# Retention's values by seven products instead of eight, with stored operand sums, in a two-block transformer kernel

## Chip, core and metric

The kernel runs on one NeuronCore of a Trainium2 chip. The metric is the time of one execution on the device in microseconds (us). PE is the matmul engine, ACT the scalar engine, DVE the vector engine, POOL the GpSimd engine; SP is the engine whose queue issues nearly all DMAs.

## What is computed

Two transformer blocks run over 512 tokens of width 1024 in fp32, and all large products are with weights that are read from HBM. Block 1 (a hybrid mixer and a feed-forward network, "ffn" here) stands ahead of the change. Block 2 has two layers of this form:

```python
mod = c_act @ w_ada + b_ada                      # "ada": per layer 3 rows of 1024
shift, scale, gate = jnp.split(mod, 3, axis=-1)
h = rmsnorm(x, norm_w) * (1.0 + scale[:, None, :]) + shift[:, None, :]
qa, ka, va, za, qr, kr, vr, zr, ga, gr = jnp.split(h @ w_in, SPLIT_POINTS, axis=-1)
# va: 3 groups of 512 columns, values of dilated attention; vr: 1024 columns, values of retention
...
o_ret = retention(qr, kr, vr, positions, ret_gn_w)   # rotary(q), rotary(k), chunks of 128 tokens
merged = sigmoid(ga) * (y_att @ w_proj_attn) + sigmoid(gr) * (o_ret * silu(zr) @ w_proj_ret)
return x + gate[:, None, :] * (merged @ w_out)
```

## The kernel before

Every fp32 operand is held as two parts, hi (rounded by ACT) and lo (the rest, by DVE), and each product of tiles is three matmuls: hi·hi, hi·lo and lo·hi. `load_w` (L188) brings one weight tile of 128x1024 (512 KB): a DMA on SP's queue into a raw buffer (L193; two in the ordinary pool, four more while a stage lends its own), ACT's split to `wh` (L144) and DVE's to `wl` (L145). A weight serves 24 matmuls of 512 columns in the products that matter here.

The program is written out by Python code in which tasks (`spawn`) take turns with the main line: after each step of a product the main line lets tasks run that are due by a clock of modelled matmul time (a task's `pace`). A scheduler then fixes the order of the instructions on each engine, SP's queue too, and weight loads are given a higher priority there. Each queue runs in its fixed order.

The stages of a block-2 layer, in order: `strided_v` gives the values of the second and third attention group; `attention` follows, which begins with the query and key weights ("qk"); then `retention_v`, the projection `pa`, `retention`, and the gates and the output.

`strided_v` (L1059) already multiplies by `TS_` (L311), a scheme of Strassen and Winograd: the product of 512 tokens, 1024 inputs and two groups of 512 columns is cut into halves of tokens and of inputs, and seven products of halves take the place of eight. It wants sums of the halves of the operand `h` (tiles `H`, four pairs of hi and lo, made in `strided_v` from `h`) and sums of the weights (`weight_sums`, L364: loads `q`, four operations on POOL, stores to HBM). The results `X` are laid into the attention's `V` tiles by 32 small DMAs (L1092), 8 first and 24 at the end. The weight sums of layer 0 are made as a task in the ffn of block 1, those of layer 1 in the last part of layer 0 (`rt2`).

`retention_v` (L1259) in contrast is an ordinary product of 8 weights, called twice a layer: the first half of the columns ahead of `pa`, the second inside `retention`. The rotary tables (`rotary_tables`, L1014; DVE work and two ACT operations that each change ACT's function table) are made in layer 0's `attention`, next to the join of its heads.

`ada` (L647) is a task in the ffn: 12 half rows, for each 8 weight pieces `aw` of 256 KB that DVE accumulates (L660), then two matmuls against a matrix of ones sum over the partitions.

Of the kernel before, what the change touches and what calls it, by code (L numbers as in the profile page):

```python
# [50 lines left out]
class Block:  # L51
# [309 lines left out]
        product("b", Sx(2), Tx(2), False, p7)  # L361
        product("a", Sx(3), B(1, 1), True, p3)

    def weight_sums(self, src, dst, pool, pace):  # L364

        g = self.nc.gpsimd
        for i in range(2):
            for o in (slice(0, 512), slice(512, D)):
                q = []
                for half, c in ((0, i), (1, i), (1, 2 + i), (0, 2 + i)):  # L370
                    q.append(pool.tile([P, 512], F32, tag=f"q{len(q)}", name=self.nm("q"), bufs=1))
# [12 lines left out]
    def all_weight_sums(self, l, pool, pace):  # L384
        A = self.A
        for n, src in (("va", [A["w2_va"][l, g] for g in (1, 2)]),):
            self.w_sums[n, l] = self.dp.tile([8, P, D], F32, tag=f"{n}{l}", name=f"{n}{l}")
            yield from self.weight_sums(src, self.w_sums[n, l], pool, pace)

    def room(self, x):  # L390

# [54 lines left out]
    def run(self):  # L446
        tc, nc, A = self.tc, self.nc, self.A
        with ExitStack() as es:
            self.es = es
            pool = lambda name, **kw: es.enter_context(tc.tile_pool(name=name, bufs=kw.pop("bufs", 1), **kw))  # L450
            self.cp = pool("const")
            self.smp = pool("small", bufs=12)
            self.es_ps = None
            self.psum(ps=8)
            self.hp = pool("h")
            self.dp = pool("dram", space=bass.MemoryType.DRAM)
            self.ident = self.cp.tile([P, P], F32, name="ident")
# [5 lines left out]
            self.cact = self.cp.tile([P, 8], F32, tag="cact", name="cact")  # L463
# [172 lines left out]
        v.tensor_add(self.merged[i], self.merged[i], T)  # L636


    def ada_init(self):
        nc, A = self.nc, self.A  # L640
        c = self.const("c_2")
        nc.scalar.activation(self.cact, c, AF.Tanh, scale=0.5)
        nc.vector.scalar_tensor_tensor(self.cact, self.cact, 1.0, c, op0=ALU.add, op1=ALU.mult)
        nc.vector.tensor_scalar(self.cact, self.cact, 0.5, None, op0=ALU.mult)
        self.ada_rows = self.dp.tile([6, D], F32, tag="adar", name="adar")

    def ada(self, pool, pace):  # L647

        nc, A, v = self.nc, self.A, self.nc.vector
        ones = pool.tile([P, P], F32R, tag="ones", name="onesr")  # L650
        nc.scalar.activation(ones, self.ones, AF.Copy)
        for l, j in [(l, j) for l in range(2) for j in range(6)]:
            o = slice(j * 512, j * 512 + 512)
            acc = pool.tile([P, 512], F32, tag="acc", name=self.nm("acc"), bufs=2)
            v.memset(acc, 0.0)
            nc.sync.dma_start(out=acc[0:1, :], in_=A["b_ada_2"][l:l + 1, o])
            for k in range(8):
                w = pool.tile([P, 512], F32, tag="aw", name=self.nm("aw"), bufs=5)
                nc.sync.dma_start(out=w, in_=A["w_ada_2"][l, k * P:(k + 1) * P, o])
# [8 lines left out]
            nc.scalar.activation(acc[0:1], ps[0:1], AF.Copy, bias=1.0 if j // 2 == 1 else 0.0)  # L668
            nc.sync.dma_start(out=self.ada_rows[l * 3 + j // 2:l * 3 + j // 2 + 1, (j % 2) * 512:(j % 2) * 512 + 512], in_=acc[0:1])


    def rnn_init(self):
# [148 lines left out]
    def ffn(self, hf, fp, es_w):  # L821
# [33 lines left out]
    def next_norm(self, l, op, pool):  # L855
# [51 lines left out]
    def block2(self, h, es_w):  # L907
# [6 lines left out]
        for l in range(2):  # L914
# [17 lines left out]
                self.attention(l, h, ap, vp, V, ya, mrg)  # L932
            e_v.close()
            with tc.tile_pool(name="retv", bufs=1, side="right", reuse_waits="tile") as rv:
                W = self.retention_v(l, h, rv, 0)
                for c in range(4):
                    w = self.load_w(A["w2_pa"][l, c])
                    for i in (2 * c, 2 * c + 1):
# [2 lines left out]
                e_ya.close()  # L941
                yo, e_yo = op("yro")
                yr = self.new_op(yo, "yr")
                with tc.tile_pool(name="ret", bufs=1, reuse_waits="tile") as rp:
                    self.retention(l, h, rp, rv, W, yr)
            mo, e_mo = op("mop")
            m = self.new_op(mo, "mo")
            with tc.tile_pool(name="rt2", bufs=1, side="right", reuse_waits="tile") as rp:
                T = {}
                if l == 0:  # L950
                    self.spawn(self.all_weight_sums(1, rp, (6.0, 9.0, 5.0)))
                for i in range(11):
                    c = i - 3
                    if i < 8:
# [56 lines left out]
            e_yo.close()  # L1011
        self.fill_up(self.cp, 448)

    def rotary_tables(self, rp):  # L1014

        nc, A, v = self.nc, self.A, self.nc.vector
        pos = rp.tile([P, S], I32, tag="qk", name="pos", bufs=4)
# [3 lines left out]
        a, k, m = (rp.tile([P, S], F32, tag="qk", name=n, bufs=4) for n in ("ra", "rk", "rm"))  # L1021
        v.tensor_copy(a, pos)
        v.tensor_scalar(a, a, th, None, op0=ALU.mult)

# [34 lines left out]
    def strided_v(self, l, h, vp, V, sp):  # L1059

        nc, v, g_ = self.nc, self.nc.vector, self.nc.gpsimd
        for g in (1, 2):
            for c in range(4):
                V[g, c] = vp.tile([P, 512], F32, tag="V", name=self.nm("V"), bufs=12)
        x_ = lambda: sp.tile([P, S], F32, tag="X", name=self.nm("X"), bufs=8)
        R, H = {}, {}
        for p in range(2):
# [13 lines left out]
        for j in (1, 0, 2, 3):  # L1081
            for p in range(2):
                o = slice(p * 512, p * 512 + 512)
                self.split(H[j][0][:, o], H[j][1][:, o], R[p][j])

        def done(t, half, z):
            x = z
            if t < 2 and half == 0:
# [2 lines left out]
            for c in range(4):  # L1091
                nc.sync.dma_start(out=V[1 + half, c][t * 32:t * 32 + 32, :], in_=x[c:P:4, :])  # L1092

        self.TS_(h, [self.A["w2_va"][l, g] for g in (1, 2)], self.w_sums["va", l],
                 lambda j, k, t, lo: H[j][lo][:, k * 256 + t * P:k * 256 + t * P + P], x_, done)

    def attention(self, l, h, ap, vp, V, ya, mrg):

# [157 lines left out]
        self.wait()  # L1256


    def retention_v(self, l, h, rv, half):  # L1259
        V = []  # L1260

        def done(t, ps):
            vt = rv.tile([P, 2, 512], F32R, tag="V", name=self.nm("V"), bufs=4)
            self.split(vt[:, 0, :], vt[:, 1, :], ps)
            V.append(vt)

        self.T_(self.tok(h), self.A["w2_vr"][l, half], 8, done, outer=2)
        return V

    def retention(self, l, h, rp, rv, V, yr):  # L1270
# [387 lines left out]
def cols(vec, n=None):  # L1658

    return np.ascontiguousarray(vec.reshape(-1, P).T)  # L1660


def prep(inp):
# [80 lines left out]
    o["c_2"] = cols(I["c_2"][0])  # L1744
    o["w_ada_2"], o["b_ada_2"] = I["w_ada_2"], I["b_ada_2"]
# [26 lines left out]
```

## Time and profile before

| | |
|---|---|
| time, median of 3 runs | 2508.74 us (2506.1 to 2509.05) |
| the profiled execution | 2508.13 us, of which the span from the first to the last instruction is 2506.3 us |
| mean granted PE clock | 0.999 of full speed |
| PE busy | 2483.5 us, 11802 matmuls |
| DVE, ACT, POOL busy | 1469.9, 1081.4 and 179.0 us |

The profile is of one execution; a sum of its parts is made against its own 2508.13 us.

### The profile page before, as it was taken

Reading aid. Unit: us, or ns where it says so; the run is one execution under the profiler, and the core shown is the slowest. Engines: PE = TensorE matmul, PEld = TensorE weight load, DVE = VectorE, ACT = ScalarE, POOL = GpSimd, SP = SyncE. Lnnn points to the kernel's source line nnn. Section 1 sums busy time; section 2 is a strip of 40 time slices with the busy share of each in tenths; the row PEclk is TensorE's granted clock in tenths of the full one; section 3 lists DMA queues with packets and bytes.
Section 4 is the critical chain, followed back from the end, with each engine's and each line's share of the span. In section 5 each row is a group of like instructions: output and inputs, shape, how many; then the busy total and the mean of one; then the engine's idle time right before and its main releaser. Section 6 shows DMA issues by size and latency. Waiting matters only on the chain.

```text
span 2506.3 us, 31435 instructions
## 1 busy us (share of the span) xinstructions
PE 2483.5 (99%) x11802; PEld 2047.5 (82%) x11802; DVE 1469.9 (59%) x2719; ACT 1081.4 (43%) x1852; POOL 179.0 (7%) x152
## 2 busy tenths in 40 slices
PE   9999999999999999999999999999999999999998
PEld 7877777888888888888888788888888888888887
DVE  6567665776656787626633536765484343375635
ACT  4477666875334333324443532333253344223323
POOL 0023332000000110001100000003020000000000
PEclk9999999999999999999999999999999999999999
DMA  6522222223345886544432222226454222322233
GB/s 183 173 79 78 72 70 93 93 91 110 118 130 173 269 273 211 183 139 141 165 119 92 63 87 82 91 78 219 147 171 154 90 84 63 98 76 93 68 101 118
DMA packets 110074, 309.54 MB, mean 124 GB/s; under 512 B 14409, under 2 KB 20425, under 8 KB 109794
## 3 DMA queue, kind: packets, MB, share of 16 engines
q1 hardware_dynamic: 109200, 306.29, 38.1%
q8 instruction: 92, 1.51, 0.3%
q10 hardware_dynamic: 722, 1.25, 0.1%
q14 instruction: 60, 0.49, 0.1%
HBM read 273.84 MB, written 21.00 MB: 118 GB/s over the span
## 4 chain that ended last, share of the span: by engine, by line
PE 89%; DVE 4%; ACT 3%; DMA 2%; issue 1%; POOL 1%; SPq 0%; ACTq 0%; DVEq 0%; POOLq 0%
PE ps L129 86%; PE ps L138 3%; DVE wl L145 1%; DMA wr<-in_w_out_dram 1%; ACT S L1534 1%; ACT wh L144 1%; DMA wr<-in_w_o_dram 0%; DVE H L145 0%; DVE yr L145 0%; POOL X L1077 0%; DVE PTl L145 0%; DVE S L1528 0%; DMA wr<-in_w_v_dram 0%; POOL S L1541 0%; ACT S L1539 0%
## 5 line engine op out<-in xcount | busy, mean ns | idle before, releaser
L129 PE MATMUL ps<-h,wh 128*128 128x512 f32 (+1 forms) x4000 | 1244.4, 391 | 0.0
L129 PEld LDWEIGHTS ps<-h,wh 128*128 128x128 f32 x4000 | 734.7, 188 | 139.5 <-issue 5.1
L145 DVE TENSOR_TENSOR wl<-wr,wh 128x1024 fp32r<-128x1024 f32 x395 | 492.6, 1250 | 486.9 <-ACT wh L144 486.5
L129 PE MATMUL ps<-h,wl 128*128 128x512 f32 (+1 forms) x2000 | 774.0, 387 | 0.1
L144 ACT ACTIVATE wh<-wr 128x1024 fp32r<-128x1024 f32 x395 | 417.3, 1059 | 807.0 <-PE ps L129 627.9
L129 PEld LDWEIGHTS ps<-h,wl 128*128 128x128 f32 x2000 | 376.2, 188 | 75.4 <-DVE wl L145 0.5
L129 PE MATMUL ps<-wh,h 128*128 128x512 f32 x672 | 211.6, 392 | 0.0
L129 PEld LDWEIGHTS ps<-wh,h 128*128 128x128 f32 x672 | 126.3, 188 | 27.0 <-DVE h L145 0.8
L129 PE MATMUL ps<-wl,h 128*128 128x512 f32 x336 | 131.5, 391 | 0.9 <-DVE wl L145 0.9
L129 PE MATMUL ps<-y,wh 128*128 128x512 f32 x384 | 119.4, 391 | 0.0
L129 PE MATMUL ps<-wh,f 128*128 128x512 f32 x288 | 89.7, 390 | 0.0
L1541 POOL TENSOR_SCALAR S<-S,sm 128x128 f32<-128x128 f32 (+3 forms) x64 | 69.6, 1099 | 213.6 <-ACT Q L144 77.7
L129 PEld LDWEIGHTS ps<-y,wh 128*128 128x128 f32 x384 | 71.5, 188 | 14.3
L375 POOL TENSOR_TENSOR q<-q,q 128x512 f32<-128x512 f32 x8 | 11.8, 1474 | 950.9 <-DMA q<-in_w_va_dram 950.9
L129 PE MATMUL ps<-yr,wh 128*128 128x512 f32 x256 | 78.8, 389 | 0.0
L660 DVE SCALAR_TENSOR_TENSOR acc<-aw,cact,acc 128x512 f32<-128x512 f32 x96 | 75.7, 790 | 5.1 <-issue 2.3
L1534 ACT ACTIVATE S<-S,sm 128x128 f32<-128x128 f32 (+3 forms) x128 | 70.2, 550 | 19.1 <-DVE sm L1532 18.8
L145 DVE TENSOR_TENSOR PTl<-ps,PTh 128x512 fp32r<-128x512 f32 (+1 forms) x96 | 65.1, 684 | 22.5 <-ACT PTh L144 21.6
L144 ACT ACTIVATE PTh<-ps 128x512 fp32r<-128x512 f32 (+1 forms) x96 | 56.0, 588 | 49.1 <-PE ps L138 43.9
L1131 DVE CUSTOM_DVE_ANT_0 P<-ps,c_masks 128x128 f32<-128x128 f32 (+1 forms) x96 | 31.2, 325 | 76.3 <-PE ps L129 74.1
L129 PEld LDWEIGHTS ps<-wl,h 128*128 128x128 f32 x336 | 63.2, 188 | 14.5 <-DVE wl L145 1.9
L129 PE MATMUL ps<-y,wl 128*128 128x512 f32 x192 | 74.8, 390 | 0.0
(362 smaller groups left out, 3331.7 us busy)
## 6 DMA issues: line engine op xcount, KB each, us to landing
aw<-in_w_ada_dram SPq DMA_DIRECT2D x96, 256.0 KB, 4.3
wr<-in_w_qk_dram SPq DMA_DIRECT2D x48, 512.0 KB, 3.5
wr<-in_w_ffn_in_dram SPq DMA_DIRECT2D x44, 512.0 KB, 3.9
wr<-in_w_g_dram SPq DMA_DIRECT2D x32, 512.0 KB, 3.5
wr<-in_w_qr_dram SPq DMA_DIRECT2D x32, 512.0 KB, 3.4
wr<-in_w_mg_dram SPq DMA_DIRECT2D x24, 512.0 KB, 3.5
wr<-in_w_ffn_out_dram SPq DMA_DIRECT2D x22, 512.0 KB, 3.9
wr<-in_w_va_dram SPq DMA_DIRECT2D x20, 512.0 KB, 5.6
```

Of the source, the lines that this page charges most:

```text
L129: self.nc.tensor.matmul(out, a, b, start=start, stop=stop, skip_group_check=True)
L138: self.nc.tensor.transpose(out, in_, self.ident[:k, :k])
L144: nc.scalar.activation(hi, src, AF.Copy)
L145: nc.vector.tensor_sub(lo, src, hi.bitcast(F32))
L375: g.tensor_sub(b11, b12, b11)
L660: v.scalar_tensor_tensor(acc, w, self.cact[:, k:k + 1], acc, op0=ALU.mult, op1=ALU.add)
L1131: v.tensor_tensor_reduce(dst, pv, mask, 1.0, -3e38, ALU.add, ALU.max, mx[:, n:n + 1])
L1534: nc.scalar.activation(Ps[h], Ps[h], AF.Exp, scale=0.125, bias=nm_[:, h:h + 1], accum_out=ls[:, h:h + 1])
L1541: nc.gpsimd.tensor_scalar(Ps[h], Ps[h], r[:, h:h + 1], None, op0=ALU.mult)
```

## The change

`retention_v` now uses `TS_`, once a layer, for both halves: 14 weights and 168 matmuls instead of 8 weights (4 for each half) and 192 matmuls. It needs the same operand sums as `strided_v`, so `strided_v` stores its eight `H` tiles to HBM (`h_sums`, task `keep`) and `retention_v` loads them again. The second half of its result goes to HBM (`vdr`) and is loaded in `retention`. The weight sums of `vr` are made too: for layer 0 in the ffn behind those of `va` (8 rounds instead of 4), for layer 1 in layer 0's `retention`, in pieces half as wide. `ada` handles four half rows in one tile (the host lays out `w_ada` for it): 3 tiles instead of 12, and 6 matmuls instead of 24, with the same 96 pieces `aw`. The rotary tables are made at the end of layer 0's `retention_v`.

```diff
-    def weight_sums(self, src, dst, pool, pace):
+    def weight_sums(self, src, dst, pool, pace, w=512):
...
-            for o in (slice(0, 512), slice(512, D)):
+            for o in (slice(a, a + w) for a in range(0, D, w)):
...
     def ada(self, pool, pace):
-        ones = pool.tile([P, P], F32R, tag="ones", name="onesr")
-        nc.scalar.activation(ones, self.ones, AF.Copy)
-        for l, j in [(l, j) for l in range(2) for j in range(6)]:
+        ones = pool.tile([P, 4], F32R, tag="ones", name="onesr")
+        nc.scalar.activation(ones, four, AF.Copy)
+        for q in range(3):
...
-            for k in range(8):
+            for k in range(32):
...
-            self.mm(ps, ones, hi, True, False)
-            self.mm(ps, ones, lo, False, True)
+            self.mm(ps[:4], ones, hi, True, False)
+            self.mm(ps[:4], ones, lo, False, True)
...
-                self.spawn(self.ada(pool[0], 1.2))
+                self.spawn(self.ada(pool[0], 1.9))
                 self.w_sums = {}
-                self.spawn(self.all_weight_sums(0, pool[0], (12.0, 16.0, 12.0)))
+                self.spawn(self.value_sums(0, ("va", "vr"), pool[0], (7.0, 9.0, 6.0)))
...
-                W = self.retention_v(l, h, rv, 0)
+                with tc.tile_pool(name="vrs", bufs=1, reuse_waits="tile") as vs:
+                    self.rawp = vs
+                    W = self.retention_v(l, h, rv, vs)
+                    self.rawp = None
...
+                    if l == 0:
+                        self.spawn(self.value_sums(1, ("vr",), rq, (4.0, 5.0, 4.0), 256), 20.0)
                     self.retention(l, h, rp, rv, W, yr)
...
     def strided_v(self, l, h, vp, V, sp):
...
+        def keep():
+            yield 12.0
+            for j in (1, 0, 2, 3):
+                for x, y in zip(H[j], self.h_sums[j]):
+                    nc.sync.dma_start(out=y, in_=x.bitcast(F32))
+                    yield 2.0
+
+        kept = self.spawn(keep())
...
+        self.wait(kept)
...
     def attention(self, l, h, ap, vp, V, ya, mrg):
...
-        if l == 0:
-            self.rotary_tables(ap)
...
-    def retention_v(self, l, h, rv, half):
-        V = []
-
-        def done(t, ps):
-            vt = rv.tile([P, 2, 512], F32R, tag="V", name=self.nm("V"), bufs=4)
-            self.split(vt[:, 0, :], vt[:, 1, :], ps)
-            V.append(vt)
-
-        self.T_(self.tok(h), self.A["w2_vr"][l, half], 8, done, outer=2)
+    def retention_v(self, l, h, rv, vs):
+        nc = self.nc
+        self.vdr = self.dp.tile([4, P, D], F32, tag="vdr", name=self.nm("vdr"))
+        V = [rv.tile([P, 2, 512], F32R, tag="V", name=self.nm("V"), bufs=4) for _ in range(4)]
+        H = {}
+        for j in (1, 0, 2, 3):
+            H[j] = [vs.tile([P, D], F32R, tag="H", name=self.nm("H"), bufs=6) for _ in range(2)]
+            for x, y in zip(H[j], self.h_sums[j]):
+                nc.sync.dma_start(out=x.bitcast(F32), in_=y)
+
+        def done(t, half, z):
+            if half == 0:
+                self.split(V[t][:, 0, :], V[t][:, 1, :], z)
+                return
+            y = vs.tile([P, 2, 512], F32R, tag="Y", name=self.nm("Y"), bufs=2)
+            self.split(y[:, 0, :], y[:, 1, :], z)
+            nc.sync.dma_start(out=self.vdr[t], in_=y.rearrange("p a b -> p (a b)").bitcast(F32))
+
+        self.TS_(h, [self.A["w2_vr"][l, i] for i in range(2)], self.w_sums["vr", l],
+                 lambda j, k, t, lo: H[j][lo][:, k * 256 + t * P:k * 256 + t * P + P],
+                 lambda: vs.tile([P, S], F32, tag="X", name=self.nm("X"), bufs=6), done)
+        if l == 0:
+            self.rotary_tables(vs, "X", 6)
         return V
...
-        Vs[1] = self.retention_v(l, h, rv, 1)
+        Vs[1] = [rv.tile([P, 2, 512], F32R, tag="V", name=self.nm("V"), bufs=4) for _ in range(4)]
+        for t, x in enumerate(Vs[1]):
+            nc.sync.dma_start(out=x.rearrange("p a b -> p (a b)").bitcast(F32), in_=self.vdr[t])
```

The new stores also change what the scheduler makes of the end of `strided_v`. SP's queue there in layer 0, before (the last of the first 8 DMAs into `V`, four weights of qk, then 24 DMAs into `V`, of which the first and the last stand here, and the next qk weights):

```order
L1092 DMA V_10916<-X_11095 32x512
L193 DMA wr_11305<-in_w_qk_dram 128x1024
L193 DMA wr_11338<-in_w_qk_dram 128x1024
L193 DMA wr_11371<-in_w_qk_dram 128x1024
L193 DMA wr_11421<-in_w_qk_dram 128x1024
L1092 DMA V_10913<-X_10969 32x512
...
L1092 DMA V_10920<-X_10972 32x512
L193 DMA wr_11454<-in_w_qk_dram 128x1024
```

The same place of the changed program (the two `va` weights are the last of `strided_v`, `hsums` the new stores):

```order
L1115 DMA V_10877<-X_11059 32x512
L193 DMA wr_11211<-in_w_va_dram 128x1024
L1104 DMA hsums_10882<-H_10905 128x1024
L193 DMA wr_11229<-in_w_va_dram 128x1024
L1104 DMA hsums_10882<-H_10906 128x1024
L193 DMA wr_11275<-in_w_qk_dram 128x1024
L193 DMA wr_11308<-in_w_qk_dram 128x1024
L1115 DMA V_10874<-X_10931 32x512
...
L1115 DMA V_10881<-X_10934 32x512
L193 DMA wr_11341<-in_w_qk_dram 128x1024
```

The last two `va` weights moved from ahead of the first 8 DMAs to behind them, and the third and fourth qk weight from ahead of the 24 DMAs to behind them. Layer 1 has the same two orders.

DVE's queue at the same place, before (`wl` is the lo split of a weight, here of the first, second and third qk weight; L346 to L349 finish the tiles `X` that the 24 DMAs read):

```order
L145 TENSOR_TENSOR wl_11308<-wr_11305,wh_11307 128x1024
L145 TENSOR_TENSOR wl_11341<-wr_11338,wh_11340 128x1024
L346 TENSOR_TENSOR X_10973<-X_10969,ps_11101 128x512
L346 TENSOR_TENSOR X_10974<-X_10970,ps_11102 128x512
L347 TENSOR_TENSOR X_10969<-X_10973,ps_11015 128x512
L347 TENSOR_TENSOR X_10970<-X_10974,ps_11016 128x512
L349 TENSOR_TENSOR X_10973<-X_10973,ps_11141 128x512
L349 TENSOR_TENSOR X_10974<-X_10974,ps_11142 128x512
L145 TENSOR_TENSOR wl_11374<-wr_11371,wh_11373 128x1024
```

And in the changed program (the first row is the lo split of the last `va` weight):

```order
L145 TENSOR_TENSOR wl_11232<-wr_11229,wh_11231 128x1024
L346 TENSOR_TENSOR X_10935<-X_10931,ps_11065 128x512
L347 TENSOR_TENSOR X_10931<-X_10935,ps_10977 128x512
L346 TENSOR_TENSOR X_10936<-X_10932,ps_11066 128x512
L349 TENSOR_TENSOR X_10935<-X_10935,ps_11107 128x512
L145 TENSOR_TENSOR wl_11278<-wr_11275,wh_11277 128x1024
L347 TENSOR_TENSOR X_10932<-X_10936,ps_10978 128x512
L145 TENSOR_TENSOR wl_11311<-wr_11308,wh_11310 128x1024
```

The operations that finish the first `X` tiles (L346, L347) moved from behind the lo splits of the first two qk weights to the place right behind the split of the last `va` weight.

## Rows read from the trace of the kernel before

**Rows 1.** Page, part 1: busy time, share of the span, instructions.

```profile
PE 2483.5 (99%) x11802; PEld 2047.5 (82%) x11802; DVE 1469.9 (59%) x2719; ACT 1081.4 (43%) x1852; POOL 179.0 (7%) x152
```

**Rows 2.** Timeline of PE in the ffn: start, us, instruction, count.

```profile
1129.78 0.62 PE L129 MATMUL ps<-wh,f 128*128 128x512 f32 x2
1130.23 0.39 PE L129 MATMUL ps<-wl,f 128*128 128x512 f32 x1
1130.46 0.62 PE L129 MATMUL ps<-wh,f 128*128 128x512 f32 x2
```

**Rows 3.** Waits of PE: total us, times, longest us.

```profile
PE ps L129 <- DMA row<-in_g_pre_mix_dram: 2.2, 1, 2.2
...
PE ps L138 <- ACT t L1182: 1.4, 1, 1.4
```

**Rows 4.** Windows: busy us by engine, PE clock, DMA share, GB/s.

```profile
1211.00:1241.00 30.00, 29.58 (x131) 24.14 (x130) 24.59 (x29) 14.59 (x17) 0.00 (x0) 1.00 0.53 169
1403.00:1441.00 38.00, 36.39 (x208) 29.92 (x208) 18.32 (x36) 20.28 (x29) 0.00 (x0) 1.00 0.13 42
1441.00:1560.00 119.00, 119.00 (x562) 99.35 (x561) 52.80 (x76) 33.79 (x44) 0.00 (x0) 1.00 0.28 89
```

**Rows 5.** Timeline of PE at the start of qk, layer 0.

```profile
1240.42 0.62 PE L129 MATMUL ps<-h,wh 128*128 128x512 f32 x2
...
1251.30 0.62 PE L129 MATMUL ps<-h,wh 128*128 128x512 f32 x2
```

**Rows 6.** Timeline of SP's queue, end of strided_v, layer 0.

```profile
1218.23 6.28 SPq L1092 DMA_DIRECT2D V<-X  x8
1224.61 10.99 SPq L193 DMA_DIRECT2D wr<-in_w_qk_dram  x4
1237.07 15.12 SPq L1092 DMA_DIRECT2D V<-X  x24
1252.29 1.00 SPq L193 DMA_DIRECT2D wr<-in_w_qk_dram  x2
```

**Rows 7.** Timeline of DVE at the same place.

```profile
1234.02 1.23 DVE L145 TENSOR_TENSOR wl<-wr,wh 128x1024 fp32r<-128x1024 f32 x1 [1.97 <-ACT wh L144]
1235.17 1.28 DVE L346 TENSOR_TENSOR X<-X,ps 128x512 f32<-128x512 f32 x2
1236.36 1.28 DVE L347 TENSOR_TENSOR X<-X,ps 128x512 f32<-128x512 f32 x2
```

**Rows 8.** Page, part 6: DMA issues, KB each, median us from issue to landing.

```profile
wr<-in_w_qk_dram SPq DMA_DIRECT2D x48, 512.0 KB, 3.5
...
wr<-in_w_va_dram SPq DMA_DIRECT2D x20, 512.0 KB, 5.6
```

**Rows 9.** Page, part 5: the splits of a weight, busy us and mean ns.

```profile
L145 DVE TENSOR_TENSOR wl<-wr,wh 128x1024 fp32r<-128x1024 f32 x395 | 492.6, 1250 | 486.9 <-ACT wh L144 486.5
...
L144 ACT ACTIVATE wh<-wr 128x1024 fp32r<-128x1024 f32 x395 | 417.3, 1059 | 807.0 <-PE ps L129 627.9
```

**Rows 10.** Timeline of SP's queue, end of strided_v, layer 1.

```profile
1879.95 5.83 SPq L1092 DMA_DIRECT2D V<-X  x8
...
1899.06 15.56 SPq L1092 DMA_DIRECT2D V<-X  x24
1914.71 1.00 SPq L193 DMA_DIRECT2D wr<-in_w_qk_dram  x2
```

**Rows 11.** Timeline of PE at the start of qk, layer 1.

```profile
1902.24 0.62 PE L129 MATMUL ps<-h,wh 128*128 128x512 f32 x2
```

**Rows 12.** Windows at PE's last matmul and behind it, columns as in rows 4.

```profile
2499.00:2500.00 1.00, 0.52 (x5) 0.31 (x3) 0.63 (x3) 0.00 (x0) 0.00 (x0) 1.00 0.35 137
...
2502.00:2503.00 1.00, 0.00 (x0) 0.00 (x0) 0.47 (x1) 0.92 (x1) 0.00 (x0) 0.74 0.00 0
```

**Rows 13.** Windows of the ffn with and without weight sums, columns as in rows 4.

```profile
840.00:860.00 20.00, 20.00 (x90) 16.57 (x89) 17.69 (x24) 7.89 (x12) 0.00 (x0) 1.00 0.94 309
...
960.00:980.00 20.00, 20.00 (x90) 16.57 (x89) 13.62 (x19) 7.48 (x10) 0.00 (x0) 1.00 0.64 207
```

More of the change, by code (lines that the diff above doesn't have):

```diff
@@ L362, in TS_ @@
         product("a", Sx(3), B(1, 1), True, p3)
[L364 removed]
+    def weight_sums(self, src, dst, pool, pace, w=512):
         g = self.nc.gpsimd
         for i in range(2):
[L368 removed]
+            for o in (slice(a, a + w) for a in range(0, D, w)):
                 q = []
                 for half, c in ((0, i), (1, i), (1, 2 + i), (0, 2 + i)):
[L371 removed]
+                    q.append(pool.tile([P, w], F32, tag=f"q{len(q)}", name=self.nm("q"), bufs=1))
                     self.nc.sync.dma_start(out=q[-1], in_=src[half][c][:, o])
@@ L382, in weight_sums, with value_sums @@
                 yield pace[2]
-    def all_weight_sums(self, l, pool, pace):
+    def value_sums(self, l, names, pool, pace, w=512):
         A = self.A
-        for n, src in (("va", [A["w2_va"][l, g] for g in (1, 2)]),):
+        src = dict(va=[A["w2_va"][l, g] for g in (1, 2)], vr=[A["w2_vr"][l, g] for g in range(2)])
+        for n in names:
             self.w_sums[n, l] = self.dp.tile([8, P, D], F32, tag=f"{n}{l}", name=f"{n}{l}")
-            yield from self.weight_sums(src, self.w_sums[n, l], pool, pace)
+            yield from self.weight_sums(src[n], self.w_sums[n, l], pool, pace, w)
     def room(self, x):
@@ L462, in run @@
             nc.vector.memset(self.ones, 1.0)
-            self.cact = self.cp.tile([P, 8], F32, tag="cact", name="cact")
+            self.fill_up(self.cp, 64)
             self.xd = [self.dp.tile([S, D], F32, tag=f"xd{i}", name=f"xd{i}") for i in range(3)]
@@ L636, in br_add, with ada_init @@
         v.tensor_add(self.merged[i], self.merged[i], T)
-    def ada_init(self):
-        nc, A = self.nc, self.A
-        c = self.const("c_2")
+    def ada_init(self, pool):
+        nc = self.nc
+        c, self.cact = (pool.tile([P, 32], F32, tag=n, name=n) for n in ("c_2", "cact"))
+        nc.sync.dma_start(out=c, in_=self.A["c_2"])
         nc.scalar.activation(self.cact, c, AF.Tanh, scale=0.5)
@@ L649, in ada @@
         nc, A, v = self.nc, self.A, self.nc.vector
-        ones = pool.tile([P, P], F32R, tag="ones", name="onesr")
-        nc.scalar.activation(ones, self.ones, AF.Copy)
-        for l, j in [(l, j) for l in range(2) for j in range(6)]:
-            o = slice(j * 512, j * 512 + 512)
+        four = pool.tile([P, 4], F32, tag="four", name="four")
+        nc.sync.dma_start(out=four, in_=A["four"])
+        ones = pool.tile([P, 4], F32R, tag="ones", name="onesr")
+        nc.scalar.activation(ones, four, AF.Copy)
+        rows = self.ada_rows.rearrange("r (a c) -> (r a) c", c=512)
+        for q in range(3):
             acc = pool.tile([P, 512], F32, tag="acc", name=self.nm("acc"), bufs=2)
             v.memset(acc, 0.0)
-            nc.sync.dma_start(out=acc[0:1, :], in_=A["b_ada_2"][l:l + 1, o])
-            for k in range(8):
+            nc.sync.dma_start(out=acc[:4], in_=A["b_ada_2"][4 * q:4 * q + 4, :])
+            for k in range(32):
                 w = pool.tile([P, 512], F32, tag="aw", name=self.nm("aw"), bufs=5)
-                nc.sync.dma_start(out=w, in_=A["w_ada_2"][l, k * P:(k + 1) * P, o])
+                nc.sync.dma_start(out=w, in_=A["w_ada_2"][q, k])
                 v.scalar_tensor_tensor(acc, w, self.cact[:, k:k + 1], acc, op0=ALU.mult, op1=ALU.add)
@@ L665, in ada @@
             ps = self.pst()
-            self.mm(ps, ones, hi, True, False)
-            self.mm(ps, ones, lo, False, True)
-            nc.scalar.activation(acc[0:1], ps[0:1], AF.Copy, bias=1.0 if j // 2 == 1 else 0.0)
-            nc.sync.dma_start(out=self.ada_rows[l * 3 + j // 2:l * 3 + j // 2 + 1, (j % 2) * 512:(j % 2) * 512 + 512], in_=acc[0:1])
+            self.mm(ps[:4], ones, hi, True, False)
+            self.mm(ps[:4], ones, lo, False, True)
+            nc.scalar.activation(acc[:4], ps[:4], AF.Copy)
+            nc.sync.dma_start(out=rows[4 * q:4 * q + 4, :], in_=acc[:4])
     def rnn_init(self):
@@ L943, in block2 @@
                 yr = self.new_op(yo, "yr")
-                with tc.tile_pool(name="ret", bufs=1, reuse_waits="tile") as rp:
+                with tc.tile_pool(name="ret", bufs=1, reuse_waits="tile") as rp, \
+                        tc.tile_pool(name="rq", bufs=1, side="right", reuse_waits="tile") as rq:
+                    if l == 0:
+                        self.spawn(self.value_sums(1, ("vr",), rq, (4.0, 5.0, 4.0), 256), 20.0)
                     self.retention(l, h, rp, rv, W, yr)
@@ L1012, in block2, with rotary_tables @@
         self.fill_up(self.cp, 448)
-    def rotary_tables(self, rp):
+    def rotary_tables(self, rp, tag, bufs):
         nc, A, v = self.nc, self.A, self.nc.vector
-        pos = rp.tile([P, S], I32, tag="qk", name="pos", bufs=4)
+        pos = rp.tile([P, S], I32, tag=tag, name="pos", bufs=bufs)
         nc.sync.dma_start(out=pos, in_=A["positions_2"].partition_broadcast(P))
@@ L1020, in rotary_tables @@
         nc.sync.dma_start(out=th, in_=A["theta"])
-        a, k, m = (rp.tile([P, S], F32, tag="qk", name=n, bufs=4) for n in ("ra", "rk", "rm"))
+        a, k, m = (rp.tile([P, S], F32, tag=tag, name=n, bufs=bufs) for n in ("ra", "rk", "rm"))
         v.tensor_copy(a, pos)
@@ L1064, in strided_v @@
                 V[g, c] = vp.tile([P, 512], F32, tag="V", name=self.nm("V"), bufs=12)
+        self.h_sums = self.dp.tile([4, 2, P, D], F32, tag="hsums", name=self.nm("hsums"))
         x_ = lambda: sp.tile([P, S], F32, tag="X", name=self.nm("X"), bufs=8)
@@ L1743, in prep @@
     o["ret_gn"] = np.stack([cols(I["ret_gn_w_2"][l]) for l in range(2)])
-    o["c_2"] = cols(I["c_2"][0])
-    o["w_ada_2"], o["b_ada_2"] = I["w_ada_2"], I["b_ada_2"]
+    o["w_ada_2"] = np.ascontiguousarray(I["w_ada_2"].reshape(2, 32, 32, 6, 512).transpose(0, 3, 1, 2, 4).reshape(
+        3, 4, 32, 32, 512).transpose(0, 2, 3, 1, 4)).reshape(3, 32, P, 512)
+    o["b_ada_2"] = I["b_ada_2"].reshape(12, 512)
+    o["c_2"] = np.repeat(np.ascontiguousarray(I["c_2"][0].reshape(32, 32).T), 4, axis=0)
+    o["four"] = np.tile(np.eye(4, dtype=f), (32, 1))
     w2 = I["nsa_wk2"][0].reshape(2, P, 64).transpose(1, 0, 2)
```

8 lines of the change are left out of this document (5 added, 3 removed).

## The prediction

> **What bounds the kernel now.** I read the page's busy shares first: PE is busy in 2483.5 of 2506.3 us, the next engine, DVE, in 59% [rows 1]. That alone doesn't say that PE sets the time, so the timeline of PE comes next. Three matmuls of 512 columns take from 1129.78 to 1130.46, so 0.227 us from one start to the next [rows 2], although each shows as 0.39 us long: they overlap, and the spacing is the price of a matmul, not its duration. The same spacing stands at the qk weights, 48 matmuls between 1240.42 and 1251.30 [rows 5]. The list of PE's waits has nothing above 2.2 us [rows 3], and a stretch of 119 us in the attention's and retention's weights shows 119.00 us busy [rows 4]. So a matmul less is 0.227 us less as long as weights keep arriving in time, and a weight that comes late costs its full delay. Both halves of this decide the change.
>
> **The change part by part.**
>
> *Matmuls.* A layer's values of retention took 8 weights at 24 matmuls, 192; seven products take 14 weights at 12, 168. That is 24 less a layer, 48 in all. `ada` goes from 24 to 6 matmuls, 18 less. Together 66 x 0.227 = **15.0 us**, and nothing covers them, since PE is the engine that is full.
>
> *Rotary tables.* The join of the heads in layer 0 waits 1.4 us for ACT's `t` [rows 3], which stands behind the second table change that `rotary_tables` brings to ACT's queue; moved away, the wait should go: **-1.4 us** (bounds 0 and -1.4). At their new place they meet the next point.
>
> *The stage of retention's values.* `TS_` brings DVE 24 more operations on `X` of 128x512 (0.64 us by the pairs in [rows 7], so 15 us in two layers) and twelve lo splits of 1.25 us, ACT twelve hi splits of 1.06 [rows 9]. Before, DVE is busy 18.3 of the 38 us that hold the first half, and the DMAs carry 42 GB/s [rows 4]; loads of `H` (4 MB) and six more weights fit under that. The nearest row is `strided_v`, the same scheme with more work around it (DVE 24.6 of 30 us, 169 GB/s): PE lost 0.42 us there [rows 4]. For 38 us that is 0.5 a layer; I take **+0.9 us** in all (0 to 3).
>
> *Weight sums and ada in the ffn.* Their matmuls are counted above; the 96 pieces `aw` stay. Eight rounds take the place of four, each with eight transfers of 256 KB (2.1 MB) in 22 us of pace: 95 GB/s. Weights and `aw` alone draw 207 GB/s, and 309 GB/s were carried in 20 us with PE full all along [rows 13]. 302 GB/s lies below that, so I cost it at nothing; the rival below says what it costs if that cover fails. The sums in layer 0's `retention` (32 loads and 32 stores of 128 KB, 8 MB over about 100 us) come on top of 89 GB/s [rows 4], and POOL, busy 179 us in all [rows 1], has nothing else there: nothing.
>
> *The end of `strided_v`.* Here the change has a price that isn't in its text. SP's queue takes 15.12 us to issue the 24 DMAs into `V` [rows 6], and whatever stands behind them waits that long. Before, four qk weights stood ahead of them; now two do, and the third comes after the 24th. PE reaches the third weight 10.88 us after the first, at 1251.30 [rows 5] (in the times of before, which hold up to there but for what was saved earlier).
>
> When do the 24 start? They wait for the first tile `X`, and SP must have issued two qk weights, the second of which needs the raw buffer of the last `va` weight. Before, that `X` came at about 1237.0, since L346 and L347 stood behind the split of the second qk weight at 1234.02 [rows 7]. Now they stand right behind the split of the last `va` weight, but this weight is issued later: behind the first 8 DMAs, which end at 1218.23 + 6.28 = 1224.5 [rows 6], one `va` weight and one store, so at about 1225.4. It lands after 3.5 us (the median of qk) to 5.6 (that of `va`) [rows 8]; with new stores between I take 4.8: 1230.2. Then hi 1.06 and lo 1.25 [rows 9]: 1232.5. Then L346 and L347 at 0.64 each: 1233.8. So the 24 start at about 1233.8, three us earlier than before, and end at 1248.9. The third qk weight is issued at 1249.0, lands 3.5 later, is split by 1253.6: 2.3 us too late. PE then does two matmuls (0.45 us) and waits for the lo part, which is 1.25 behind: 0.8 more. **+3.1 us** in layer 0. Queued behind the late weight are only the following ones, which have 24 matmuls of time each and catch up.
>
> Layer 1 has the same order. The first 8 end at 1879.95 + 5.83 = 1885.8 [rows 10]; with the same 9.3 us from there the 24 start at 1895.1 and end 15.56 later at 1910.7; weight ready at 1915.3, wanted at 1902.24 + 10.88 = 1913.1 [rows 10, 11]: 2.2 + 0.8, **+3.0 us**.
>
> The bounds: if the 24 start no earlier than before, the third weight is issued at 1252.29 and 1914.71 [rows 6, 10], and the stalls are 6.35 and 6.95, 13.3 in all; if the last `va` weight lands after 3.5 us they are 1.3 us smaller each, 3.5 in all; if something else lets the weight come early, 0.
>
> *The clock.* A PE that waits may be clocked down. It ran at full clock through its longest wait at work, 2.2 us [rows 3]; its last matmul ends at about 2499.5, and from 2502 to 2503, with no matmul, the granted clock is 0.74 of full, so it fell to the lower level, 1.2 GHz, within that us [rows 12]. The stalls that I expect (2.3 us, two matmuls, 0.8 us) lie between. No row shows matmuls at the lower level; with the 24 of the late weight at half clock each stall would cost up to 5.4 more, without it 0. The stall is nearest to the 2.2 us wait, so I take 0. The Trainium skill (TensorE: Matmul & The Clock Gate, Part 1: The HAM clock gate) has it that the throttled state is the default and activity releases it; by that rule a stall that is long enough is paid twice, and the sum would be up to 10.8 us higher, 2510 instead of 2499.3. The trace agrees as far as it goes: the clock falls after PE has stopped, and not in the short wait.
>
> *Sum:* 2508.13 - 15.0 - 1.4 + 0.9 + 3.1 + 3.0 = 2498.7 for the profiled execution, which lies 0.6 below the median of the runs: **2499.3**, say 2499.5.
>
> **The rivals.**
>
> *A. The weights aren't late.* If the third qk weight is there in time, 2508.13 - 15.0 - 1.4 + 0.9 are left, 2492.6, and with the 0.6 to the median 2493.2. For it: every estimate of the stall is a difference of two chains of some ten steps, and 2 us less on each settles it. Against: 15 us of issuing on one queue are seen twice [rows 6, 10]. Chance 0.15.
>
> *B. The 24 DMAs start as late as before*, and the stalls are 13.3: 2505.9 + 0.6 = 2506.5, and 2508 to 2512 if the clock falls too, which waits of 5.6 us make likely. That is no change that can be measured: what a run of this kernel tells from no change is about 0.2%, 5.0 us. For it: the new stores share the DMAs with the last `va` weights just there, at a share of 0.53 already [rows 4]. Against: DVE's new order, which takes the first `X` ahead of the qk splits. Chance 0.22.
>
> *C. The ffn becomes bound by its DMAs* and the kernel slower. Some 180 us of ffn now ask for 302 GB/s all along, where 309 were seen for 20 us at a share of 0.94 [rows 13], so there is little above it. If the DMAs sustain only 270, the stage grows by 12% of 180, 21 us: 2520. It ends slower from the point at which the growth beats 9.4 (down to no change) plus 5.0, 14.4 us, which is a sustained rate of 280 GB/s. Against: PE was full in that window with DVE at 17.7 of 20 us, and the weights run ahead of their use. Chance 0.10.
>
> **How the numbers follow.** The forecast has 0.53, with a range of its own from 2495 to 2504; its upper edge is the bound of faster (2503.7). A is faster as well. B is the same, but for a small part; C is slower or, if mild, the same. So faster 0.65, same 0.24, slower 0.11. The range that leaves no more than 2 in 10 out reaches from A to B with the clock's price: 2492 to 2511.
>
> **What the changed profile would show.** 66 matmuls fewer of 512 columns, at the same 0.227 us. In SP's timeline the first 8 DMAs into `V` end near 1224 (less what was saved in `ada`, 4 us), 24 more start 9 us later, and the third qk weight follows them. In PE's waits two entries of 2 to 3 us on ACT's `wh` or on a qk weight, with 0.8 us on `wl` behind each, one in each layer at the start of attention; the 1.4 us on `t` gone. If the entries are 5 us and more, B holds, and the granted clock in the us behind them says whether it fell. If there are none, A. In the ffn PE should stay full in every window of 20 us; one with less than 19.5 speaks for C. The forecast is wrong if the stage of retention's values shows waits that sum to more than 3 us, or if the rows of SP in `retention` show its weights stuck behind rounds of `q`.

## The result, and the profile after

The changed kernel takes 2524.64 us (median of 6 runs, 2522.98 to 2525.58) against 2508.70 before: a ratio of 1.0066 with a 95% interval from 1.0056 to 1.0077, so **16 us slower**. The forecast was 2499.5, faster, with a range up to 2511. The profiled execution took 2524.04 us.

Part 1 of the page, as in [rows 1]:

```profile
PE 2477.8 (98%) x11736; PEld 2038.9 (81%) x11736; DVE 1501.2 (60%) x2737; ACT 1084.7 (43%) x1848; POOL 235.0 (9%) x200
```

The 66 matmuls are gone. That the span grew all the same must show as waits of PE; the list of these (total us, times, longest), as in [rows 3]:

```profile
PE ps L129 <- ACT wh L144: 13.1, 4, 6.9
PE ps L129 <- ACT rh L144: 10.2, 3, 9.4
```

Two kinds of wait are new. The first, on a weight's hi split, is the one forecast at the end of `strided_v`, but more than twice as long. The second, on `rh`, the rotated queries and keys of retention, was not forecast. SP's queue at the first place, layer 0, as in [rows 6]:

```profile
1212.54 6.76 SPq L1115 DMA_DIRECT2D V<-X  x8
1219.39 0.53 SPq L193 DMA_DIRECT2D wr<-in_w_va_dram  x1
1219.96 0.43 SPq L1104 DMA_DIRECT2D hsums<-H  x1
1220.49 0.38 SPq L193 DMA_DIRECT2D wr<-in_w_va_dram  x1
1220.91 1.12 SPq L1104 DMA_DIRECT2D hsums<-H  x1
1222.14 7.59 SPq L193 DMA_DIRECT2D wr<-in_w_qk_dram  x2
1230.71 15.53 SPq L1115 DMA_DIRECT2D V<-X  x24
1246.33 8.02 SPq L193 DMA_DIRECT2D wr<-in_w_qk_dram  x4
```

ACT's splits of the last `va` weight (first row) and of the third qk weight:

```profile
1227.04 1.06 ACT L144 ACTIVATE wh<-wr 128x1024 fp32r<-128x1024 f32 x1 [1.94 <-DMA wr<-in_w_va_dram]
...
1250.45 1.06 ACT L144 ACTIVATE wh<-wr 128x1024 fp32r<-128x1024 f32 x1 [3.94 <-DMA wr<-in_w_qk_dram]
```

PE at the third qk weight, and the windows around it (columns as in rows 4):

```profile
1245.49 0.39 PE L129 MATMUL ps<-h,wl 128*128 128x512 f32 x1
1251.56 1.22 PE L129 MATMUL ps<-h,wh 128*128 128x512 f32 x2 [5.68 <-ACT wh L144]
1252.81 0.79 PE L129 MATMUL ps<-h,wl 128*128 128x512 f32 x1
```

```profile
1245.00:1250.00 5.00, 0.87 (x4) 0.38 (x2) 0.00 (x0) 0.60 (x1) 0.00 (x0) 0.95 0.63 214
1250.00:1255.00 5.00, 3.41 (x7) 2.31 (x8) 2.45 (x2) 2.11 (x2) 0.00 (x0) 0.50 0.32 104
1255.00:1260.00 5.00, 5.00 (x21) 3.85 (x21) 2.63 (x10) 2.12 (x2) 0.00 (x0) 0.87 0.42 152
```

The order is the one read ahead of the run: 24 DMAs between the second and the third weight, 15.5 us. The last `va` weight was issued at 1220.49 and split only at 1227.04, 6.55 us later, so the 24 began 11.4 us after the first 8 had ended, not 9.3. PE stood for 5.7 us, and when work came the granted clock was 0.50: two matmuls fill 1.22 us where they filled 0.62 in [rows 5]. In layer 1 the last `va` weight took 8.3 us to its split, the 24 began 13.2 us after the 8, and PE waited 6.9 us.

SP's queue ahead of the wait on `rh`, in layer 0's `retention` (`q` and `vr` are the loads and stores of the weight sums for layer 1):

```profile
1576.67 0.42 SPq L193 DMA_DIRECT2D wr<-in_w_qr_dram  x1
1579.07 2.94 SPq L381 DMA_DIRECT2D vr<-q  x4
1582.12 1.85 SPq L372 DMA_DIRECT2D q<-in_w_vr_dram  x4
1586.50 5.06 SPq L381 DMA_DIRECT2D vr<-q  x4
1591.66 1.83 SPq L372 DMA_DIRECT2D q<-in_w_vr_dram  x4
1596.12 1.92 SPq L381 DMA_DIRECT2D vr<-q  x3
1598.09 0.43 SPq L193 DMA_DIRECT2D wr<-in_w_qr_dram  x1
```

PE behind it:

```profile
1593.83 0.39 PE L129 MATMUL ps<-h,wl 128*128 128x512 f32 x1
1603.65 0.80 PE L129 MATMUL ps<-rh,rh 128*128 128x512 f32 x1 [9.44 <-ACT rh L144]
```

A late weight makes `rh` late by way of ACT's queue, in which the split into `rh` stands behind the split of that weight, although DVE had finished what `rh` is made from at 1591.77:

```profile
1602.02 1.06 ACT L144 ACTIVATE wh<-wr 128x1024 fp32r<-128x1024 f32 x1 [14.10 <-DMA wr<-in_w_qr_dram]
1602.98 0.61 ACT L144 ACTIVATE rh<-ra 128x512 fp32r<-128x512 f32 x1
```

Between the weights at 1576.67 and 1598.09 stand two and a half rounds, 21 us. A weight gives PE 5.45 us of matmuls, and the operations between them don't fill 21. A round holds SP because its stores wait for POOL's sums, and the loads of the next round stand behind the stores. Of SP's waits from 1535 to 1612 (total us, times, longest), the stores' for POOL sum to 35.3 us in four entries, of which the largest is

```profile
SPq L381 <- POOL q L375: 18.3, 8, 3.5
```

The clock falls in this wait as well; it is at 0.50 where PE goes on (columns as in rows 4):

```profile
1605.00:1610.00 5.00, 4.24 (x10) 3.09 (x11) 3.38 (x5) 0.63 (x1) 3.04 (x3) 0.50 0.35 111
```

To see what each place costs in all, the clock too, I count between the same two matmuls of both traces. From the first qk matmul to the start of a later stretch of 47 qk matmuls, PE needs 8.4 us more than before in layer 0 and 9.3 in layer 1, **17.7** together, of which 13.7 are gaps between the starts of matmuls beyond their usual spacing (5.8 and 7.1 on `wh`, 0.4 and 0.4 on `wl` right behind it) and 4.0 lie behind them, where the clock is low. From the weights of the second head of `retention` to the stretch behind the wait, it needs **13.9** more, clock included.

### The profile page after: what moved, and what is told of

The parts are those of the page before. It is cut to its first block, busy times and chain, and to the rows that moved or that the text cites. A ratio compares the mean times of both kernels' runs of the same rounds, so it can differ in the third digit from the quotient of the medians.

```text
span 2522.2 us, 31589 instructions
## 1 busy us (share of the span) xinstructions
PE 2477.8 (98%) x11736; PEld 2038.9 (81%) x11736; DVE 1501.2 (60%) x2737; ACT 1084.7 (43%) x1848; POOL 235.0 (9%) x200
## 5 line engine op out<-in xcount | busy, mean ns | idle before, releaser
L145 DVE TENSOR_TENSOR wl<-wr,wh 128x1024 fp32r<-128x1024 f32 x407 | 507.8, 1253 | 475.5 <-ACT wh L144 474.9
L144 ACT ACTIVATE wh<-wr 128x1024 fp32r<-128x1024 f32 x407 | 429.1, 1058 | 777.7 <-PE ps L129 495.2
L129 PE MATMUL ps<-wh,h 128*128 128x512 f32 x512 | 162.5, 395 | 0.3 <-ACT h L144 0.3
L375 POOL TENSOR_TENSOR q<-q,q 128x512 f32<-128x512 f32 (+1 forms) x20 | 26.4, 1319 | 984.9 <-DMA q<-in_w_vr_dram 432.0
L129 PEld LDWEIGHTS ps<-wh,h 128*128 128x128 f32 x512 | 96.9, 190 | 21.2 <-DVE h L145 0.8
L129 PE MATMUL ps<-wl,h 128*128 128x512 f32 x256 | 100.7, 393 | 0.9 <-DVE wl L145 0.9
L667 DVE SCALAR_TENSOR_TENSOR acc<-aw,cact,acc 128x512 f32<-128x512 f32 x96 | 84.9, 884 | 24.9 <-DMA aw<-in_w_ada_dram 23.0
L129 PE MATMUL ps<-wh,H 128*128 128x512 f32 x256 | 79.5, 389 | 0.0
L1567 DVE CUSTOM_DVE_ANT_0 S<-ps,c_mask 128x128 f32<-128x128 f32 (+3 forms) x128 | 59.9, 482 | 8.6 <-PE ps L129 7.4
```

The lines of the kernel that those rows point to most:

```text
L129: self.nc.tensor.matmul(out, a, b, start=start, stop=stop, skip_group_check=True)
L144: nc.scalar.activation(hi, src, AF.Copy)
L145: nc.vector.tensor_sub(lo, src, hi.bitcast(F32))
L1567: v.tensor_tensor_reduce(Pt[:, o], ps[:, o], self.mask[:, 512 - N:], 1.0, -3e38, ALU.add, ALU.max, mx[:, h:h + 1])
```

## The experiments

Beside each of these runs the kernel before ran too; its medians lie between 2507.68 and 2508.70 us, so about 1 us between two of these runs says nothing.

**The 24 DMAs on another queue.**

```diff
-                nc.sync.dma_start(out=V[1 + half, c][t * 32:t * 32 + 32, :], in_=x[c:P:4, :])
+                g_.dma_start(out=V[1 + half, c][t * 32:t * 32 + 32, :], in_=x[c:P:4, :])
```

> The changed kernel with the 32 DMAs from X into V of strided_v issued on POOL's queue instead of SP's; same bytes, same stores of H. Theory: in the changed kernel the third qk weight stands on SP's queue behind 24 of these DMAs, and by PE's progress against the kernel before, the two places cost 8.4 us (layer 0) and 9.3 us (layer 1). Without them in the way both waits on wh at the start of attention go, and the time falls by about 17.7 us, from 2524.6 to about 2507. Rival: the stores of H load the DMA engines so that the weight lands late; then the bytes are the same, the waits stay, and the time stays within 4 us of 2524.6.

2517.86 us: 6.8 less, not 17.7. The waits on `wh` are gone (0.5 us is the longest left), though the stores of `H` still go by SP's queue just ahead of the qk weights, so it is not their load on the DMAs that held the weight; but another wait took their place (PE):

```profile
1256.78 1.23 PE L129 MATMUL ps<-qk,qk 128*128 128x128 f32 x4 [4.37 <-ACT qk L1170]
```

The scores wait for ACT's evictions of the first products, which now stand behind the splits of four weights, some with a late DMA:

```profile
1254.70 1.06 ACT L144 ACTIVATE wh<-wr 128x1024 fp32r<-128x1024 f32 x1 [2.01 <-DMA wr<-in_w_qk_dram]
1255.66 1.06 ACT L1170 ACTIVATE qk<-ps 128x512 f32<-128x512 f32 x2
```

The experiment moved too much: it changed ACT's order with SP's. It speaks against the rival and does not by itself prove the size.

**The rounds in another stage.**

```diff
-                        self.spawn(self.value_sums(1, ("vr",), rq, (4.0, 5.0, 4.0), 256), 20.0)
...
-                    self.spawn(self.value_sums(1, ("va",), rp, (6.0, 9.0, 5.0)))
+                    self.spawn(self.value_sums(1, ("vr", "va"), rp, (4.0, 7.0, 4.0)))
```

> The changed kernel with the weight sums of vr for layer 1 made in the last part of layer 0 (with those of va, 8 rounds of 512 columns) instead of in layer 0's retention. Theory: in retention SP's queue holds weights of qr behind the stores of a round, which wait for POOL, and that costs 13.9 us by PE's progress; without the rounds there the wait of 9.4 us on rh goes and the time falls to about 2511, if the longer row of rounds in the last part costs nothing (0 to 4 us). Rival: the retention stage is late for another reason (DVE's operations beside POOL, the late second half of the values), and the wait stays: 2522 to 2525.

2519.90 us, 4.7 less. The wait on `rh` is gone, as expected, but eight rounds in the last part hold up the weights of `w_out`, which follow them on SP (PE):

```profile
1804.11 2.80 PE L129 MATMUL ps<-yr,mo 128*128 128x512 f32 x11 [1.74 <-DVE yr L145]
...
1817.44 0.80 PE L129 MATMUL ps<-wh,mo 128*128 128x512 f32 x1 [3.16 <-ACT wh L144]
```

(`yr` is here the room in which a weight of `w_out` is split.) The rounds took their price along.

**The stores alone, on the kernel before.** In `strided_v` of the kernel before:

```diff
+        kept = self.spawn(keep())
...
+        self.wait(kept)
```

> The kernel before with one part of the change alone: strided_v stores its eight H tiles to HBM (16 stores of 512 KB in two layers), and nothing reads them. Theory: the stores alone turn the order of SP's queue at the end of strided_v, and with it come two waits of 5.8 and 7.1 us at the third qk weight and the lower clock behind them, 17.7 us in all: about 2526. Rival: the waits need more than that (other late buffers of the changed stage), and the time is 2509 to 2512.

2525.73 us, 17.1 more than before (ratio 1.0071, 1.0056 to 1.0086). The waits, with the same line on top as in the changed kernel:

```profile
PE ps L129 <- ACT wh L144: 12.4, 4, 5.9
```

So 16 stores that nobody reads explain the first place: 17.1 of its 17.7 us.

**The waits filled with matmuls.** In `attention`, ahead of the third qk weight:

```diff
+                    if (hd, g, j) == (0, 1, 0):
+                        f = self.pst()
+                        for _ in range(20):
+                            nc.tensor.matmul(f, h.h(0, 0, P), h.h(0, 0, S), start=True, stop=True, skip_group_check=True)
```

> The changed kernel with 20 matmuls of 512 columns ahead of the third qk weight in each layer, on operands that are there and into a bank that nothing reads: 4.5 us of PE's time each, inside the waits of 5.8 and 7.1 us. Theory on the clock: the wait lets the granted clock fall to half, and the matmuls behind it pay 2.1 us (layer 0) and 1.8 to 2.2 us (layer 1); with the wait filled the clock stays at 1.00 and the time falls by about 4 us to 2520.6. Rival: the waits are the whole price and the time stays at 2524.6 within 1 us.

2521.48 us, 3.2 less, though 40 matmuls were added. The windows at the same place:

```profile
1245.00:1250.00 5.00, 5.00 (x24) 4.14 (x23) 0.00 (x0) 0.60 (x1) 0.00 (x0) 1.00 0.49 154
1250.00:1255.00 5.00, 3.30 (x15) 2.24 (x14) 2.78 (x6) 2.12 (x2) 0.00 (x0) 1.00 0.42 134
```

The clock stays at 1.00 although a wait of 1.7 us is left here and one of 1.8 in layer 1. The lower clock cost about 3 us at the two places: 3.2 by the medians, whose runs overlap (2520.39 to 2525.09 against 2522.98 to 2525.58), and 2.7 by PE's progress from the late weight's first matmul to the same stretch of 47 (1.0 and 1.7 us).

**H stores on POOL's queue.** In `keep`:

```diff
-                    nc.sync.dma_start(out=y, in_=x.bitcast(F32))
+                    g_.dma_start(out=y, in_=x.bitcast(F32))
```

> The changed kernel with the eight H tiles of each layer stored by POOL's queue instead of SP's; the same bytes at the same points of the program. SP's queue at the end of strided_v then has the order of before: the last va weights ahead of the first 8 DMAs into V, four qk weights ahead of the 24. Theory (order of the queue): both waits at the third qk weight go, with the clock's price, and 17.7 us come back: 2507. Rival (load on the DMA engines): the same 8 MB move, and the weights are late all the same: above 2518.

2509.20 us, 15.4 less. The bytes still move, and SP's queue reads as in [rows 6]:

```profile
1224.98 9.11 SPq L193 DMA_DIRECT2D wr<-in_w_qk_dram  x4
1235.56 15.12 SPq L1115 DMA_DIRECT2D V<-X  x24
1250.78 1.00 SPq L193 DMA_DIRECT2D wr<-in_w_qk_dram  x2
```

It is the order of the queue. This run alone leaves one doubt, since on POOL's queue the stores also come earlier in layer 0, the last at 1209.65 instead of 1220.91. Two other runs settle it: with the 24 DMAs on POOL's queue (above) and with the stores on ACT's (below; four of them are issued from 1223.38 on, among the qk weights) no wait on `wh` is above 0.5 us either.

The 2.3 us that didn't come back lie, by PE's progress, at the same two places, which still need 1.9 and 1.1 us more than before. About half of that is short waits of the scores for DVE, which the kernel before doesn't have there (total us, times, longest):

```profile
PE ps L129 <- DVE mc L1155: 1.5, 3, 0.6
```

**The rounds of `retention` on POOL's queue.**

```diff
-                    self.nc.sync.dma_start(out=q[-1], in_=src[half][c][:, o])
+                    (self.nc.sync if w == 512 else g).dma_start(out=q[-1], in_=src[half][c][:, o])
...
-                    self.nc.sync.dma_start(out=dst[2 * j + i][:, o], in_=t)
+                    (self.nc.sync if w == 512 else g).dma_start(out=dst[2 * j + i][:, o], in_=t)
```

> The changed kernel with the loads and stores of the rounds in layer 0's retention (vr of layer 1, 256 columns wide) on POOL's queue. Theory: SP's queue, which holds weights of qr behind stores that wait for POOL, is what makes rh late; without the rounds on SP the wait of 9.4 us goes and 13.9 us come back: about 2511. Rival: POOL's operations themselves slow DVE, or the rounds' bytes delay the weights; both stay, and so does the wait: 2520 to 2525.

2510.97 us, 13.7 less, with POOL's sums and their bytes at the same place. SP, not POOL or the DMA engines, was the mechanism.

**Only the stores of the rounds on POOL's queue** (with the H stores there too; of the last diff only the second pair of lines).

> As the kernel with H stores and rounds on POOL's queue, but only the stores of the rounds there; their loads stay on SP, where 9 of them stand in one place ahead of a weight of qr. If it is the stores, which wait for POOL's results, that hold SP, the time is 2496. If the loads hold it as well, because each waits until the store of the round before has left its buffer, a wait on rh of some us stays and the time is 2500 to 2511.

2511.70 us, just above the range that was expected, and 2.5 above the run with the H stores moved alone: nothing came back at this place. SP, and PE behind it:

```profile
1576.75 18.73 SPq L372 DMA_DIRECT2D q<-in_w_vr_dram  x9
1595.57 0.38 SPq L193 DMA_DIRECT2D wr<-in_w_qr_dram  x1
```

```profile
1602.00 0.80 PE L129 MATMUL ps<-rh,rh 128*128 128x512 f32 x1 [13.97 <-ACT rh L144]
```

The loads hold SP as well as the stores did: with one buffer a tag, each waits until the store of the round before has left it, as SP's own waits show:

```profile
SPq L372 <- DMA vr<-q: 48.8, 21, 4.5
```

The wait is even longer, since nine of them now stand in a row.

**Both on POOL's queue:** the H stores and the rounds of `retention`, by the two diffs above.

> Both edits together: H stores and the rounds in retention on POOL's queue. If both theories hold, all but the work that the change saves is gone: 2524.6 - 17.7 - 13.9 = 2493, against 2493.2 for the rival of the prediction in which no weight is late. If POOL, which now issues 48 more DMAs in each place, gets late with work that others wait for, 2495 to 2505.

**2495.91 us** (2492.51 to 2498.79), a ratio of 0.9950 to the kernel before (0.9936 to 0.9964): faster than both. No wait of PE is above 2.7 us any more:

```profile
PE ps L129 <- DVE wl L145: 3.6, 8, 0.9
PE ps L129 <- DMA row<-in_g_pre_mix_dram: 2.7, 1, 2.7
PE ps L129 <- ACT rh L144: 2.0, 2, 1.0
```

**A dose: three qk weights ahead.** As the last, with the H stores on ACT's queue; the scheduler then puts three weights ahead of the 24.

```diff
-                    g_.dma_start(out=y, in_=x.bitcast(F32))
+                    nc.scalar.dma_start(out=y, in_=x.bitcast(F32))
```

> As the kernel with H stores and rounds on POOL's queue, but the H stores on ACT's queue. SP's queue then has three qk weights ahead of the 24 DMAs into V, not four and not two: the fourth comes behind them. By the theory a weight moved ahead buys 24 matmuls, 5.45 us, so that waits of 5.8 and 7.1 us at the third weight become 0.4 and 1.6 us at the fourth, with no time for the clock to fall: 2 us more than with four ahead, 2496 to 2499. Rival: what matters is only how loaded the DMA engines are, and then it is as with the stores on POOL within 1 us, or ACT's own queue, with 8 issues more, is late with splits: above 2500.

2498.45 us, 2.5 more than with four:

```profile
1224.66 9.21 SPq L193 DMA_DIRECT2D wr<-in_w_qk_dram  x3
1234.86 15.13 SPq L1115 DMA_DIRECT2D V<-X  x24
1250.09 8.09 SPq L193 DMA_DIRECT2D wr<-in_w_qk_dram  x4
```

PE's waits at the fourth weight are 0.5 us (layer 0) and 0.6 (layer 1), both on `wl`, and the granted clock there stays at 1.00. With the rounds on POOL's queue, two weights ahead cost 15.1 us more than four (2510.97 against 2495.91), three 2.5: the third buys 5.45 us of matmuls in each layer and keeps the clock up. The two kernels' runs overlap (2495.37 to 2498.99 here), so the 2.5 are no more than in line with it.

**Rotary alone, on the kernel before** (made behind the first call of `retention_v`).

> The kernel before with one part of the change alone: the rotary tables are made at the end of the first call of retention_v in layer 0 instead of in attention. Theory: the wait of 1.4 us on t at the join goes, and the time falls by 1.4 to 2.2 us (2.2 is what PE gained over that stretch in the changed kernel), to about 2506.7. Rival: the work waits elsewhere, behind the values' splits on ACT, and the time is the same within 0.5 us.

2505.05 us, 2.9 less (ratio 0.9991, 0.9981 to 1.0000). The wait on `t` is gone from the list.

**`ada` alone, on the kernel before.**

> The kernel before with one part of the change alone: ada by four half rows to a tile, 18 matmuls fewer. Theory: 18 x 0.227 = 4.1 us less, 2503.8, since PE is full in the ffn on both sides. Rival: DVE's 96 operations, now slower paced, or the longer task cost the gain elsewhere: 2507 to 2509.

2503.77 against 2507.68, 3.9 less (ratio 0.9983, 0.9974 to 0.9992), for 18 matmuls, 4.1 us.

## Why the prediction was wrong, step by step

*Matmuls, -15.0: right as far as it was isolated.* `ada` alone gave 3.9 of its 4.1 us, and with both waits out of the way the kernel is 12.0 us faster than before. The 4.4 us that lack to 16.4 (the rotary tables' 1.4 included) are no more than what that run's trace shows elsewhere: PE needs 1.7 and 1.0 us more than before at the starts of attention, and waits 2.3 us on `rh` and `rl` in layer 0's `retention`. The 48 matmuls of `retention_v` had no run of their own.

*Rotary, -1.4: right in kind*; alone it gave 2.9 us with an interval that reaches to nothing, and 2.2 by PE's progress over that stretch of the changed kernel.

*The stage of retention's values, +0.9: it cost nothing.* PE is full through layer 0's, from 1477.6 to 1515.4 and on into `pa` (columns as in rows 4), and waits nowhere in layer 1's:

```profile
1477.00:1537.00 60.00, 60.00 (x267) 49.69 (x266) 45.64 (x61) 26.78 (x31) 0.00 (x0) 1.00 0.61 203
```

The 38 us that the prediction read for the stage, 1403 to 1441 in [rows 4], are not it: there the attention's heads are joined, and the matmuls of the first half ran from 1477.1 to 1498.8. The term came out near by luck, not by that row.

*Weight sums in the ffn, 0: right, and rival C false.* PE was full in each window of 20 us from 800 to 1000, even in this one:

```profile
860.00:880.00 20.00, 20.00 (x90) 16.57 (x89) 16.17 (x20) 6.37 (x8) 5.82 (x4) 1.00 0.98 359
```

The DMAs carry more than the 309 GB/s that were taken for near the top.

*Weight sums in layer 0's `retention`, "nothing": this is the step that failed.* It weighed the rounds on POOL and on the DMA engines' bandwidth, where they are free indeed, and left out the third thing that they use, SP's queue, on which the weights stand behind them. The last sentence of the prediction names the sign, "its weights stuck behind rounds of `q`", but no term and no rival stood for it. It cost 13.9 us by PE's progress and 13.7 by moving the rounds off SP. Without it the changed kernel lands at 2511, the upper edge of the stated range, as the run with the rounds on POOL's queue did (2510.97).

*The end of `strided_v`: the mechanism right, the size too small.* I took 3.1 + 3.0 us; the waits are 13.7 in all, near the 13.3 of rival B. The term that was mis-sized is the start of the 24 DMAs, and in it the landing of the last `va` weight. I took 4.8 us and as an upper bound 5.6, the median of before. From issue to the start of the split it took 6.55 and 8.3, with the new stores just ahead of it and behind it. The median was the wrong row: for this very weight the trace of before has, in layer 0 and without any stores,

```profile
wr<-in_w_va_dram SPq DMA_DIRECT2D x1, 512.0 KB, 6.2
```

so there the stores added little; for layer 1 before has no landing, and whether they made the 8.3 is open. The third weight's own landing took 4.1 in layer 0, not 3.5. The new DVE order, on which I relied to start the 24 early, was there, but waited for that weight.

*The clock, 0: wrong once the waits were longer.* With 5.7 and 6.9 us it fell to 1.2 GHz, and PE lost about 3 us; in `retention`, behind 9.4 us, it fell too (part of the 13.9). The row that the 0 rested on doesn't bear it: the wait of 2.2 us is no wait at work but the first 2.25 us of the span, ahead of PE's first matmul:

```profile
2.25 3.75 PE L129 MATMUL ps<-row,one 1*128 1x512 f32 x4 [2.25 <-DMA row<-in_g_pre_mix_dram]
```

The rule cited from the Trainium skill (TensorE: Matmul & The Clock Gate, Part 1: The HAM clock gate) was on the right side: the granted clock was 0.50 behind the waits and rose again under work. The 10.8 us that were worked out beside it were three times too high, since PE was back at full clock before the late weight's 24 matmuls were through.

Together, from the forecast's 2499.3: +7.6 for the waits (13.7 for 6.1), +4.0 behind them, +13.9 for `retention`, -0.9 for the stage, -0.8 for the rotary tables: 2523.1 of 2524.6. What is left over is not assigned.

## What to carry to other kernels

A new DMA is priced on three things: its bytes, the engine that makes its data, and the queue that issues it. The last is the one that bit here twice: SP's queue ran in order, so a store that waited for a result (35.3 us of waits in one stage), or a load that waited for its buffer (48.8 us where only the stores were moved), held every weight behind it. When new DMAs go into the queue that feeds a full matmul engine, read what stands behind them, how long that may be late (here 24 matmuls for each weight already there), and put them on a queue that feeds nobody. And read a landing time at the place where it counts, not as a median of its kind: for the last `va` weight that was 6.2 us against 5.6, and 6.55 and 8.3 with the new DMAs around it.

## What the hardware showed unexpectedly

- At half clock matmuls of 512 columns start 0.43 us apart (1253.40 to 1254.26 for two, in layer 0), against 0.227. The granted clock, 0.50 from 1250 to 1255, is 0.87 on average in the next five us, in which PE is full; where the same place was filled with matmuls up to waits of 1.7 and 1.8 us, it stayed at 1.00.
- A weight of 512 KB with stores of 512 KB just ahead of it and behind it took 6.55 and 8.3 us from issue to split; the same weight took 6.2 us to land in layer 0 without them, and the median of its kind was 5.6.
- POOL's queue takes DMAs in 0.55 us each beside its own operations, and with 64 of them in `retention` PE's waits on `rh` are 2.0 us in all, where they were 10.2 with these DMAs on SP's queue.
